# Block sums of the squared activations in a two-layer encoder: made beside the up projection and stored as finished operands, or made again from stored activations beside the down projection

## The chip, the cores and the metric

One of the eight cores of a Trainium2 chip runs the whole program. The metric is device time in microseconds from launch to end, and lower is better. The kernel before was run three times: 2643.0 us is the median, 2638.96 us the lowest. A further execution was recorded by the hardware profiler; the rows below come from it.

## What is computed

The reference is a two-layer encoder for 1024 tokens of width 1024. Layer 0 mixes tokens by banded attention, layer 1 by a gated delta rule. Each layer then adds a dense MLP with a squared ReLU; the change lies in these two MLPs alone.

```python
def squared_relu_mlp(h, w_up, w_down):          # w_up 1024 x 4096, w_down 4096 x 1024
    return jnp.square(jax.nn.relu(h @ w_up)) @ w_down
...
x = x + squared_relu_mlp(rmsnorm(x, mlp_norm[i]), mlp_w_up[i], mlp_w_down[i])
```

All of it is float32. The kernel reaches that precision on TensorE by writing each operand as a high part (rounded to the fp32r format) plus a low part (the rest), and multiplying high by high, high by low and low by high. So one product of two 128-wide operands is three matmuls (`block_product`, L998), and every operand needs a "high" (a ScalarE copy with rounding, `high`, L1012) and a "low" (a subtraction, `low`, L1006, on VectorE, or on GpSimd where its last argument is true).

## The kernel before

Everything is kept transposed: features on the 128 partitions, the 1024 tokens along the free dimension in two halves of 512. A tile of 128 features by 1024 tokens is 512 KB, one half of it 256 KB.

Both projections use the seven-product form of a 2x2 block product (eight products in the plain form). For the right-hand operand with blocks 11, 12, 21, 22 (first digit the half of the features, second the half of the tokens) this needs 11, 21 and 22 themselves and four block sums: t1 = 12 - 11, t2 = 22 - t1, t3 = 22 - 12, t4 = 21 - t2. The weights have their own sums s1 to s4. Results gather in PSUM banks called X (in the trace `acc`), Y and Z.

**Up projection** (`up`, L1077). Sixteen steps n; step n makes two tiles of 128 rows of h @ w_up, numbers 2n and 2n+1, in seven block products of 12 matmuls each, in the order 11, t1, t2, 21, t3, 22, t4 of the right-hand operand (from the second step on; the last has t4 before 22). While TensorE works on step n, the other engines make the weight operands of step n+1 (`up_weights`, L1026): GpSimd four sums and differences, ScalarE the highs, VectorE the lows. Bank Y takes the products 11, t2, t3 and t4 one on top of the other and is read out after each, so the next product into Y has to wait for that reading: after 11 and t2 by a ScalarE copy (`copy`, L1104, into a tile `nt`), after t3 and t4 by VectorE (`put`, L1082). `put` makes a result: VectorE adds the copied bank (L1087), then takes the ReLU and multiplies by the norm's factor R (L1089), ScalarE squares (L1090) and sends the 256 KB to DRAM (L1091, tensor `gd`). The buffers of the results are four halves called `ssum` and `g` in the trace.

**Down projection** (`down`, L1313). The 4096 rows of the activations form 8 blocks b of four tiles; each block times four pairs of output tiles u gives 32 units of seven block products of 6 matmuls. `slot` (L1366) is one product: the matmuls, then `step` (L1328), then a VectorE add of the bank onto the running result x in SBUF (L1369). Bank Y again holds four products, so the add after a product stands between it and the next product into the same bank, with one product of another bank in between to cover it. `step` advances two helpers by one stage each: `rows` (L1264), which prepares the activation operands of block b+1, and `down_weights` (L1173), which prepares the weight operands of the next unit. All engines run their own instructions strictly in program order; what `step` emits comes ahead of the add of the same slot.

`rows` loads the four 256 KB blocks 11, 12, 21, 22 from `gd`, and for each of the two tile rows j of a block makes the four sums on GpSimd (`psub`, L1015, which the trace shows at L1016), seven highs on ScalarE, and seven lows, four on VectorE and three (`PLO`, L28) on GpSimd. It takes 14 slots for one j, that is two units. `first_rows` (L1237) does the same for block 0 during the last step of the up projection, called by `tail` (L1485) in `block` (L1467), which also reloads the residual tiles x0 and x1 early and x2 to x7 at its end.

TensorE, VectorE, ScalarE and GpSimd follow the order in which the code is written (`manual_schedule`, L1500). SyncE only issues loads and stores; a scheduler orders its queue by when it takes the buffers to be free, and it waits at each entry until that entry's data and buffer are ready.

## Time and profile before

| What | Value |
|---|---|
| Median of three runs | 2643.0 us (lowest 2638.96) |
| The profiled execution | 2639.7 us |
| Span in the profile, first to last instruction | 2637.9 us (1.8 us lie outside) |
| Mean granted TensorE clock | 0.983 of full speed |
| TensorE busy | 2492.1 us, 94% of the span |
| VectorE, ScalarE, GpSimd busy | 72%, 46%, 50% |
| Moved by DMA | 271.78 MB, mean 103 GB/s |
| Up projections | about 561 to 891 us and 1953 to 2282 us |
| Down projections | about 891 to 1234 us and 2282 to 2622 us |

Times inside the trace count from the span's start. "Busy" is the time in which at least one instruction of an engine ran. A matmul's end is modelled and overlaps the start of the next, so idle time of PE in brackets is somewhat less than what a wait really cost; the distance between the starts of two matmuls shows the whole. PE is TensorE, DVE VectorE, ACT ScalarE, POOL GpSimd, SP SyncE; L161 is a recording helper that stands for many lines.

### The profile page before, as it was taken

The numbers are of one execution on the slowest core, as the hardware profiler recorded it, in microseconds if no ns is written. First come the engines' busy times: TensorE is split into PE (matmuls) and PEld (weight loads), VectorE is DVE, ScalarE is ACT, GpSimd is POOL, SyncE is SP. The second block draws the span as 40 slices with busy tenths as digits, with TensorE's granted clock in tenths as the row PEclk, the third lists the DMA queues.
The fourth block names the chain that finished last, engine by engine and source line by source line (L and its number), as shares of the span: only waits on it lengthen the run. The fifth ranks groups of instructions, "written<-read, shape, count | busy, mean of one in ns | idle before, by whom it ended". The sixth has DMA issues, their size and how long they took to land.

```text
span 2637.9 us, 36117 instructions
## 1 busy us (share of the span) xinstructions
PE 2492.1 (94%) x12638; PEld 2061.5 (78%) x12638; DVE 1886.2 (72%) x3287; ACT 1225.0 (46%) x2269; POOL 1310.9 (50%) x1100
## 2 busy tenths in 40 slices
PE   8999999989999999998888999999899999999997
PEld 6888888867888777776677788888777888777775
DVE  6665656575454899997579976666676545899997
ACT  6665667443444444434673343343334434444443
POOL 2444456242222788886464333332133232688886
PEclk9999999999999999999998999999999999999998
DMA  4222225324333423323443122223323323432322
GB/s 159 67 70 72 68 84 164 104 80 142 114 105 119 152 96 108 100 88 114 115 140 111 54 73 65 67 72 108 108 96 132 116 104 120 153 103 97 103 97 80
DMA packets 141814, 271.78 MB, mean 103 GB/s; under 512 B 49264, under 2 KB 55856, under 8 KB 141632
## 3 DMA queue, kind: packets, MB, share of 16 engines
q1 hardware_dynamic: 120752, 227.51, 27.0%
q10 hardware_dynamic: 20880, 41.97, 4.1%
q8 instruction: 99, 1.62, 0.3%
q14 instruction: 83, 0.68, 0.1%
HBM read 193.24 MB, written 67.80 MB: 99 GB/s over the span
## 4 chain that ended last, share of the span: by engine, by line
PE 70%; DVE 18%; issue 6%; ACT 3%; DMA 2%; POOL 1%; SPq 0%; ACTq 0%; DVEq 0%; POOLq 0%
PE y L1004 20%; PE acc L161 17%; PE z L1004 9%; PE acc L1004 6%; PE tp L161 3%; DVE x L1369 3%; DVE a L1010 3%; PE s L161 3%; PE po L161 2%; PE pt L161 2%; PE sp L161 2%; PE acc L276 2%; PE acc L277 2%; PE acc L275 2%; DVE ft L161 2%
## 5 line engine op out<-in xcount | busy, mean ns | idle before, releaser
L161 PE MATMUL acc<-xhi,whi 128*128 128x512 f32 (+1 forms) x904 | 372.8, 412 | 7.2 <-DVE xp L161 7.2
L161 PE MATMUL acc<-xlo,whi 128*128 128x512 f32 (+1 forms) x904 | 371.7, 411 | 0.6 <-DVE xlo L391 0.6
L161 PE MATMUL acc<-xhi,wlo 128*128 128x512 f32 x896 | 368.0, 411 | 2.8 <-POOL wlo L161 2.8
L1019 POOL TENSOR_TENSOR s<-wraw 128x256 f32<-128x256 f32 (+1 forms) x93 | 101.3, 1089 | 538.6 <-DMA wraw<-in_w_up_dram 380.0
L161 POOL TENSOR_TENSOR wlo<-wraw,whi 128x512 fp32r<-128x512 f32 x126 | 168.1, 1334 | 242.8 <-ACT whi L161 193.8
L1013 ACT ACTIVATE xhi<-r 128x512 fp32r<-128x512 f32 x224 | 135.9, 628 | 261.5 <-POOL r L1016 210.0
L1010 DVE TENSOR_TENSOR wlo<-wraw,whi 128x512 fp32r<-128x512 f32 (+1 forms) x184 | 203.4, 1105 | 50.8 <-ACT whi L1013 47.5
L1004 PE MATMUL y<-xhi,a 128*128 128x512 f32 x488 | 181.3, 412 | 33.1 <-DVE x L1369 30.4
L1004 PE MATMUL y<-xhi,wlo 128*128 128x512 f32 x504 | 200.1, 397 | 13.1 <-DVE wlo L1010 13.1
L1004 PE MATMUL y<-xhi,whi 128*128 128x512 f32 x504 | 200.3, 397 | 11.6 <-DVE ssum L1087 9.1
L1016 POOL TENSOR_TENSOR r<-r,r 128x512 f32<-128x512 f32 x124 | 204.1, 1648 | 13.6 <-DVE xlo L1010 13.3
L1004 PE MATMUL y<-xlo,whi 128*128 128x512 f32 x504 | 199.2, 395 | 0.0
L161 PEld LDWEIGHTS acc<-xhi,whi 128*128 128x128 f32 (+1 forms) x904 | 172.2, 190 | 31.9 <-DVE xp L161 4.4
L161 PEld LDWEIGHTS acc<-xhi,wlo 128*128 128x128 f32 x896 | 171.1, 191 | 28.4 <-POOL wlo L161 4.1
L161 PEld LDWEIGHTS acc<-xlo,whi 128*128 128x128 f32 (+1 forms) x904 | 172.5, 191 | 24.9 <-DVE xlo L391 1.2
L1369 DVE TENSOR_TENSOR x<-y,x 128x512 f32<-128x512 f32 x240 | 163.6, 682 | 8.9 <-PE y L1004 8.5
L1013 ACT ACTIVATE whi<-wraw 128x512 fp32r<-128x512 f32 (+2 forms) x191 | 143.7, 766 | 35.1 <-ACT g L1090 12.3
L1004 PEld LDWEIGHTS y<-xhi,a 128*128 128x128 f32 x488 | 92.0, 189 | 80.1 <-DVE x L1369 60.1
L161 POOL TENSOR_SCALAR pr<-pr,rs 128x640 f32<-128x640 f32 (+4 forms) x128 | 88.6, 696 | 128.9 <-DVE rs L161 97.9
L1087 DVE TENSOR_TENSOR ssum<-acc,nt 128x512 f32<-128x512 f32 x32 | 22.1, 690 | 175.7 <-PE acc L1004 175.7
L161 POOL TENSOR_TENSOR cy<-cy,cz 128x512 f32<-128x512 f32 x48 | 68.9, 1436 | 145.1 <-DVE cz L161 131.2
L1010 DVE TENSOR_TENSOR a<-s,a 128x256 fp32r<-128x256 f32 x117 | 129.7, 1109 | 0.0
(349 smaller groups left out, 7089.3 us busy)
## 6 DMA issues: line engine op xcount, KB each, us to landing
wraw<-in_w_up_dram SPq DMA_DIRECT2D x64, 512.0 KB, 3.3
wraw<-in_w_down_dram SPq DMA_DIRECT2D x64, 512.0 KB, 3.9
r<-gd SPq DMA_DIRECT2D x112, 256.0 KB, 2.7
gd<-ssum ACTq DMA_DIRECT2D x64, 256.0 KB, 2.0
gd<-g ACTq DMA_DIRECT2D x64, 256.0 KB, 2.2
wraw<-in_w_in_dram SPq DMA_DIRECT2D x32, 512.0 KB, 3.5
wraw<-in_w_qkv_dram SPq DMA_DIRECT2D x30, 512.0 KB, 3.4
x<-xd SPq DMA_DIRECT2D x24, 512.0 KB, 5.1
```

Of the source, the lines that this page charges most:

```text
L161: return call(*args, **more)
L275: nc.tensor.matmul(ps, hi[:, k], xh, start=(k == 0), stop=False)
L276: nc.tensor.matmul(ps, hi[:, k], xl, start=False, stop=False)
L277: nc.tensor.matmul(ps, lo[:, k], xh, start=False, stop=(k == KT - 1))
L1004: nc.tensor.matmul(ps, w[:, k], x, start=bool(first and f), stop=bool(last and e), skip_group_check=True)
L1010: self.nc.vector.tensor_tensor(lo, src, hi.bitcast(F32), ALU.subtract)
L1013: self.nc.scalar.activation(hi, src, AF.Copy)
L1016: self.nc.gpsimd.tensor_tensor(out, x, y, ALU.subtract)
L1019: self.nc.gpsimd.tensor_tensor(out, x, y, ALU.add)
L1087: nc.vector.tensor_tensor(g, c, t, ALU.add)
L1369: nc.vector.tensor_tensor(x, ps, x, ALU.add)
```

## The change

Both halves of an up step now belong to one pair of blocks: the halves of a down block are its even and its odd tiles (the reordering of w_down in `layout`), so that step n of the up projection makes all four blocks of one tile row j. A new generator `combine` makes the four sums of step n beside step n+1: GpSimd subtracts, ScalarE makes the high part, VectorE the low part in place, and one 512 KB store per sum puts high and low, side by side, into the DRAM tensor `gt`. Blocks 11, 21 and 22 are stored as before (tensor `gr`); block 12 is no longer stored. In the down projection `rows` loads the raw 11, 21 and 22 and makes their highs on ScalarE and all their lows on GpSimd; the sums are loaded straight into the operand tiles, two loads of 256 KB each. `first_rows` does likewise. High and low of an operand are now two halves of one tile. The sums of the last up step are made in the first slots of the down projection, and the residual tiles are loaded later: x0 to x3 at the end of `tail`, x4 to x7 behind those last sums.

```diff
+    def combine(self, n, g, mp, gt):
+        t = {z: mp.tile([P, S], F32, name=self.nm("c"), tag=f"x{4 * (n % 2) + k}") for k, z in enumerate(SUMS)}
+        def sub(z, x, y):
+            self.psub(t[z][:, HB:], x, y)
+        def high(z):
+            self.high(t[z][:, :HB].bitcast(F32R), t[z][:, HB:])
+        def low(z):
+            nc.vector.tensor_tensor(t[z][:, HB:].bitcast(F32R), t[z][:, HB:], t[z][:, :HB], ALU.subtract)
+            nc.sync.dma_start(gt[n, SUMS.index(z)], t[z])
+        sub("t1", g[0, 1], g[0, 0])
+        sub("t3", g[1, 1], g[0, 1])
+        yield
+        sub("t2", g[1, 1], t["t1"][:, HB:])
+        sub("t4", g[1, 0], t["t2"][:, HB:])
+        high("t1")
+        yield
+        high("t3")
+        low("t1")
+        yield
+        high("t2")
+        low("t3")
+        yield
+        high("t4")
+        low("t2")
+        yield
+        low("t4")
+        yield
...
-            nc.scalar.dma_start(gd[m, :, s], g)
+            g_of[m % 2, h] = g
+            if (m % 2, h) in RAW:
+                nc.scalar.dma_start(gr[m // 2, RAW.index((m % 2, h))], g)
...
+                next(sums)
                 self.block_product(Z, A["s1"], ops["t1"], True, False)
                 next(rest, None)
                 beside(1, lambda: next(more, None), lambda: copied("z5", Z))
+                next(sums)
                 end()
                 self.block_product(Y, A["s2"], ops["t2"], False, False)
                 copied("u2", Y)
+                next(sums)
                 end()
                 self.block_product(X, A["12"], ops["21"], True, True)
                 beside(2, lambda: next(more, None), lambda: put(2 * n, 0, X, keep["p1"]))
+                next(sums)
                 self.block_product(Y, A["s3"], ops["t3"], False, False)
                 beside(3, lambda: (next(more, None), end()), lambda: put(2 * n + 1, 1, Y, keep["z5"]))
+                next(sums)
...
+            sums = self.combine(n, dict(g_of), mp, gt)
+            if n < last:
+                next(sums)
...
+    def load_sum(self, part, src):
+        hi, lo = part
+        self.nc.sync.dma_start(hi.bitcast(F32), src[:, :HB])
+        self.nc.sync.dma_start(lo.bitcast(F32), src[:, HB:])
+    def rows(self, hx, gr, gt, b, ops):
         for j in range(2):
+            n = 2 * b + j
+            r = {}
+            for k, name in enumerate(RAWS):
+                r[name] = hx.tile([P, HB], F32, name=self.nm("r"), tag=f"a{6 + k}")
+                self.nc.sync.dma_start(r[name], gr[n, k])
+            yield
+            for k, name in enumerate(RAWS):
+                self.high(self.rows_part(hx, ops, b, name, j)[0], r[name])
+                yield
                 h, l = ops[name][j]
+                self.low(l, r[name], h, True)
+                yield
+            yield
+            for k, name in enumerate(SUMS):
+                self.load_sum(self.rows_part(hx, ops, b, name, j), gt[n, k])
+                yield
+            yield
+            yield
...
-                got["xs"] += self.load_x(xp, xd, range(2, KT))
+                got["xs"] = self.load_x(xp, xd, range(4))
+                yield
+            def late():
+                for k in range(4, KT):
+                    got["xs"] += self.load_x(xp, xd, (k,))
...
-    o["w_down"] = np.ascontiguousarray(w.transpose(0, 1, 5, 4, 6, 2, 3, 7)).reshape(2, 8, 4, P, 4, 2, P)
+    o["w_down"] = np.ascontiguousarray(w.transpose(0, 1, 5, 4, 6, 3, 2, 7)).reshape(2, 8, 4, P, 4, 2, P)
```

TensorE's instructions and their order are the same in both kernels, and over the whole program VectorE, GpSimd and ScalarE execute the same number of highs, lows and subtractions. What differs is where they stand. Three places follow. In their rows a name's number only tells buffers apart, and a line number belongs to the kernel that the row is from.

VectorE in one step of the up projection, before, from the result of product 21 to the lows of the next weights:

```order
L1087 TENSOR_TENSOR ssum_6920<-acc_8069,nt_8086 128x512
L1089 SCALAR_TENSOR_TENSOR ssum_6920<-ssum_6920,R_6907 128x512
L1087 TENSOR_TENSOR ssum_6920<-y_8070,nt_8105 128x512
L1089 SCALAR_TENSOR_TENSOR ssum_6920<-ssum_6920,R_6907 128x512
L1010 TENSOR_TENSOR alo_8137<-s_8133,ahi_8136 128x512
L1010 TENSOR_TENSOR wlo_8143<-wraw_8101,whi_8142 128x1024
L1087 TENSOR_TENSOR g_6921<-z_8071,nt_8119 128x512
L1089 SCALAR_TENSOR_TENSOR g_6921<-g_6921,R_6907 128x512
```

The same place after, with the two rows ahead of it; c is a tile of a sum, in the order t1, t3, t2, t4:

```order
L1093 TENSOR_TENSOR c_8164<-c_8164 128x512
L1093 TENSOR_TENSOR c_8166<-c_8166 128x512
L1127 TENSOR_TENSOR ssum_6864<-acc_8170,nt_8187 128x512
L1129 SCALAR_TENSOR_TENSOR ssum_6864<-ssum_6864,R_6851 128x512
L1093 TENSOR_TENSOR c_8165<-c_8165 128x512
L1127 TENSOR_TENSOR ssum_6864<-y_8171,nt_8209 128x512
L1129 SCALAR_TENSOR_TENSOR ssum_6864<-ssum_6864,R_6851 128x512
L1093 TENSOR_TENSOR c_8167<-c_8167 128x512
L1014 TENSOR_TENSOR alo_8247<-s_8243,ahi_8246 128x512
L1014 TENSOR_TENSOR wlo_8253<-wraw_8205,whi_8252 128x1024
L1127 TENSOR_TENSOR g_6865<-z_8172,nt_8226 128x512
L1129 SCALAR_TENSOR_TENSOR g_6865<-g_6865,R_6851 128x512
```

Four lows have come into the step: two while VectorE has nothing else to do, and two (t2 and t4) between the results of products 21 and 22.

GpSimd in two units of the down projection, before (s and wraw: weights; r: raw blocks; xlo: the low part of an activation operand):

```order
L1016 TENSOR_TENSOR r_9513<-r_9514,r_9513 128x512
L1008 TENSOR_TENSOR xlo_9572<-r_9513,xhi_9571 128x512
L1016 TENSOR_TENSOR r_9514<-r_9516,r_9514 128x512
L1008 TENSOR_TENSOR xlo_9595<-r_9514,xhi_9594 128x512
L1016 TENSOR_TENSOR r_9513<-r_9516,r_9513 128x512
L1019 TENSOR_TENSOR s_9617<-wraw_9600 128x256
L1016 TENSOR_TENSOR s_9618<-s_9617,wraw_9600 128x256
L1016 TENSOR_TENSOR r_9515<-r_9515,r_9513 128x512
L1016 TENSOR_TENSOR s_9617<-wraw_9600 128x256
L1016 TENSOR_TENSOR wraw_9600<-wraw_9600,s_9618 128x256
L1008 TENSOR_TENSOR xlo_9665<-r_9515,xhi_9664 128x512
```

And after, where two units hold these (xs is an operand's tile of high and low):

```order
L1023 TENSOR_TENSOR s_9721<-wraw_9700 128x256
L1020 TENSOR_TENSOR s_9722<-s_9721,wraw_9700 128x256
L1012 TENSOR_TENSOR xs_9732<-r_9712,xs_9732 128x512
L1020 TENSOR_TENSOR s_9721<-wraw_9700 128x256
L1020 TENSOR_TENSOR wraw_9700<-wraw_9700,s_9722 128x256
L1012 TENSOR_TENSOR xs_9755<-r_9714,xs_9755 128x512
L1012 TENSOR_TENSOR xs_9773<-r_9716,xs_9773 128x512
L1023 TENSOR_TENSOR s_9804<-wraw_9789 128x256
L1020 TENSOR_TENSOR s_9805<-s_9804,wraw_9789 128x256
L1020 TENSOR_TENSOR s_9804<-wraw_9789 128x256
L1020 TENSOR_TENSOR wraw_9789<-wraw_9789,s_9805 128x256
```

The four subtractions r<-r,r are gone from the two units; the three lows remain, now of the raw blocks. VectorE's four lows of activations are gone too, so that between its seven adds of a unit only the four lows of the weights stand.

SyncE's queue around the end of the first up projection, before: the loads of the first two down weights, one raw block for block 1, and residual tiles x2 to x5 (x0 and x1 were loaded 300 us earlier):

```order
L1031 DMA wraw_8798<-in_w_up_dram 128x1024
L1176 DMA wraw_8923<-in_w_down_dram 128x1024
L1176 DMA wraw_9125<-in_w_down_dram 128x1024
L1270 DMA r_9137<-gd_6121 128x512
L2449 DMA x_9117<-xd_6122 128x1024
```

And after, where c_9114, c_9113 and c_9115 are the sums t3, t2, t4 of the last but one up step, xs_9284 and xs_9287 the operands t4 of block 0, x_9314 to x_9320 the residual tiles x0 to x3, and wraw_9322 the weights of the second unit:

```order
L1094 DMA gt_6090<-c_9114 128x1024
L1337 DMA xs_9284<-gt_6090 128x512
L1094 DMA gt_6090<-c_9113 128x1024
L1338 DMA xs_9284<-gt_6090 128x512
L1337 DMA xs_9287<-gt_6090 128x512
L1094 DMA gt_6090<-c_9115 128x1024
L1338 DMA xs_9287<-gt_6090 128x512
L2505 DMA x_9314<-xd_6091 128x1024
L2505 DMA x_9316<-xd_6091 128x1024
L2505 DMA x_9318<-xd_6091 128x1024
L2505 DMA x_9320<-xd_6091 128x1024
L1227 DMA wraw_9322<-in_w_down_dram 128x1024
```

The residual tiles and the second unit's weights have come behind the stores of sums and the loads of operands.

## Rows read from the trace of the kernel before

**Rows 1.** The page: each engine's busy time with its share of the span and its instructions, and the chain of work that ended last, by engine.

```profile
PE 2492.1 (94%) x12638; PEld 2061.5 (78%) x12638; DVE 1886.2 (72%) x3287; ACT 1225.0 (46%) x2269; POOL 1310.9 (50%) x1100
PE 70%; DVE 18%; issue 6%; ACT 3%; DMA 2%; POOL 1%; SPq 0%; ACTq 0%; DVEq 0%; POOLq 0%
```

**Rows 2.** Busy time by stretch: an up and a down stretch of 50 us in the first MLP. Columns: length; PE, PEld, DVE, ACT, POOL busy with their instructions; granted clock, DMA share, GB/s.

```profile
750.00:800.00 50.00, 50.00 (x223) 41.40 (x222) 25.17 (x32) 20.81 (x33) 10.79 (x9) 1.00 0.35 122
1000.00:1050.00 50.00, 48.09 (x207) 38.07 (x206) 46.37 (x64) 20.39 (x37) 43.58 (x36) 1.00 0.29 95
```

**Rows 3.** Who waited for whom over the whole span: us in total, times, the longest.

```profile
POOL s L1019 <- DMA wraw<-in_w_up_dram: 380.0, 28, 17.9
ACT xhi L1013 <- POOL r L1016: 210.0, 112, 2.2
...
PE y L1004 <- DVE x L1369: 33.0, 34, 2.1
```

**Rows 4.** TensorE's timeline: start, duration, instruction, in brackets the idle time before it and what ended it. First the starts of product 11 in two successive up steps and of product t2 in the second of them; then product t2 in five units of the two down projections (the first unit and the 28th of each, and two units that lie two apart).

```profile
696.18 0.39 PE L1004 MATMUL y<-xhi,whi 128*128 128x512 f32 x1
...
715.22 0.39 PE L1004 MATMUL y<-xhi,whi 128*128 128x512 f32 x1
...
720.66 0.39 PE L1004 MATMUL y<-xhi,ahi 128*128 128x512 f32 x1
...
896.26 0.50 PE L1004 MATMUL y<-xhi,a 128*128 128x512 f32 x1 [2.04 <-DVE x L1369]
...
989.44 0.50 PE L1004 MATMUL y<-xhi,a 128*128 128x512 f32 x1 [0.84 <-DVE x L1369]
...
1010.21 0.50 PE L1004 MATMUL y<-xhi,a 128*128 128x512 f32 x1 [0.84 <-DVE x L1369]
...
1176.35 0.50 PE L1004 MATMUL y<-xhi,a 128*128 128x512 f32 x1 [0.84 <-DVE x L1369]
...
2287.36 0.50 PE L1004 MATMUL y<-xhi,a 128*128 128x512 f32 x1 [2.04 <-DVE x L1369]
...
2566.91 0.50 PE L1004 MATMUL y<-xhi,a 128*128 128x512 f32 x1 [0.84 <-DVE x L1369]
```

**Rows 5.** VectorE's timeline just ahead of the product at 989.44, then one ScalarE row of the same moment and the start of TensorE's product before it.

```profile
985.16 1.58 DVE L1010 TENSOR_TENSOR a<-s,a 128x512 fp32r<-128x512 f32 x1
986.66 0.68 DVE L1369 TENSOR_TENSOR x<-y,x 128x512 f32<-128x512 f32 x1
987.49 1.29 DVE L1010 TENSOR_TENSOR wlo<-wraw,whi 128x512 fp32r<-128x512 f32 x1
988.70 0.68 DVE L1369 TENSOR_TENSOR x<-y,x 128x512 f32<-128x512 f32 x1
...
986.23 0.63 ACT L1013 ACTIVATE xhi<-r 128x512 fp32r<-128x512 f32 x1 [2.13 <-POOL r L1016]
...
987.07 0.39 PE L1004 MATMUL z<-xhi,a 128*128 128x512 f32 x1
```

**Rows 6.** Groups of instructions of VectorE and GpSimd from 947.4 to 1196.6 us, six blocks of the first down projection: count, busy us, mean ns of one, idle time before them.

```profile
L1369 DVE TENSOR_TENSOR x<-y,x 128x512 f32<-128x512 f32 x97 | 66.1, 682 | 2.0 <-PE y L1004 1.9
L1010 DVE TENSOR_TENSOR wlo<-wraw,whi 128x512 fp32r<-128x512 f32 x46 | 46.1, 1002 | 1.6
L1010 DVE TENSOR_TENSOR a<-s,a 128x512 fp32r<-128x512 f32 x22 | 34.1, 1548 | 0.0
...
L1016 POOL TENSOR_TENSOR r<-r,r 128x512 f32<-128x512 f32 x46 | 76.4, 1661 | 0.0
```

**Rows 7.** The same view from 640 to 840 us, in the first up projection: lows of weight sums on VectorE, and sums of weights on GpSimd.

```profile
L1010 DVE TENSOR_TENSOR alo<-s,ahi 128x512 fp32r<-128x512 f32 x32 | 22.0, 688 | 4.5 <-ACT ahi L1013 4.5
...
L1016 POOL TENSOR_TENSOR s<-s,wraw 128x512 f32<-128x512 f32 x11 | 14.2, 1292 | 0.9
```

**Rows 8.** Timeline of one up step: four results on VectorE, and ScalarE's copy of the next step's product 11.

```profile
708.04 1.22 DVE L1089 SCALAR_TENSOR_TENSOR ssum<-ssum,R 128x512 f32<-128x512 f32 x1
710.04 0.69 DVE L1087 TENSOR_TENSOR ssum<-y,nt 128x512 f32<-128x512 f32 x1 [0.78 <-PE y L1004]
710.76 0.69 DVE L1089 SCALAR_TENSOR_TENSOR ssum<-ssum,R 128x512 f32<-128x512 f32 x1
...
715.42 0.69 DVE L1089 SCALAR_TENSOR_TENSOR g<-y,R 128x512 f32<-128x512 f32 x1 [0.30 <-PE y L1004]
...
718.25 0.58 ACT L1106 ACTIVATE nt<-y 128x512 f32<-128x512 f32 x1
```

**Rows 9.** Timeline of the last two up steps of the first MLP, where the subtractions of `first_rows` run on GpSimd: VectorE, then the waits of TensorE up to the down projection.

```profile
860.36 1.63 DVE L1089 SCALAR_TENSOR_TENSOR ssum<-ssum,R 128x512 f32<-128x512 f32 x1
...
869.35 1.78 DVE L1010 TENSOR_TENSOR alo<-s,ahi 128x512 fp32r<-128x512 f32 x1
...
874.47 0.50 PE L1004 MATMUL y<-xhi,ahi 128*128 128x512 f32 x1 [1.33 <-ACT nt L1106]
...
881.18 0.50 PE L1004 MATMUL y<-xhi,ahi 128*128 128x512 f32 x1 [0.98 <-ACT nt L1106]
...
885.76 0.50 PE L1004 MATMUL y<-xhi,whi 128*128 128x512 f32 x1 [1.56 <-DVE ssum L1087]
```

**Rows 10.** DMA: the stretch around the start of the first down projection (columns as in Rows 2), and the page's line on the loads of residual tiles (KB each, median us from issue to landing).

```profile
883.00:900.00 17.00, 13.40 (x53) 10.34 (x52) 15.52 (x24) 9.95 (x19) 4.53 (x5) 0.93 0.83 292
...
x<-xd SPq DMA_DIRECT2D x24, 512.0 KB, 5.1
```

130 lines of the change are left out of this document (55 added, 75 removed).

## The prediction

> **What bounds the kernel now.** I read the page first. TensorE is busy 94% of the span and makes 70% of the chain that ended last; VectorE makes 18% of it [rows 1]. Those are averages over stages, so I went on to busy time by stretch. In an up stretch TensorE is busy 50.00 of 50 us, with VectorE at 25 and GpSimd at 11. In a down stretch it is busy 48.1, while VectorE stands at 46.4 and GpSimd at 43.6 [rows 2]. So the up projections are bound by matmuls with room beside them, and the down projections sit at a place where three engines are almost full. The view of waits names the pair: TensorE's product into Y waits for VectorE's add onto x, 33.0 us in 34 waits [rows 3].
>
> How much that costs is read better from starts of matmuls than from the idle times, since a matmul's end is modelled. An up step has 84 matmuls and takes 715.22 - 696.18 = 19.04 us, 0.2267 us each [rows 4]. Two down units also have 84, and there the same product returns after 1010.21 - 989.44 = 20.77 us [rows 4]: 1.73 us are lost in each pair of units. From the first unit's t2 product to the 28th's lie 27 units, 1134 matmuls, 257.0 us at the up pitch; the trace shows 1176.35 - 896.26 = 280.1 in the first MLP and 2566.91 - 2287.36 = 279.6 in the second [rows 4]. The losses are 23.0 and 22.5, together 45.6 us. This is all that a better down projection could return in the stretch that the change touches; the last block, which prepares no rows, is not in it.
>
> Why the add is late is seen just ahead of 989.44 [rows 5]. VectorE takes the low of the weights s3 and s1 in 1.58 us, adds, waits, takes another low in 1.29 and only then adds what TensorE waits for. Where GpSimd rests, such a low takes 0.69 [rows 7]; in the down projection the two sorts average 1.55 and 1.00 beside GpSimd's subtractions of 1.66 us [rows 6]. An add that reads a PSUM bank stays at 0.68 there [rows 6]. ScalarE is held as well: it stands 210 us behind those subtractions [rows 3], one of them 2.13 us ahead of the very high whose low is late [rows 5].
>
> **The change, part by part.** *Down projection.* For two units it removes four subtractions of 1.66 us (6.6) from GpSimd, four lows of 0.68 (2.7) from VectorE, four highs from ScalarE, and with them the wait of ScalarE for GpSimd. What remains on VectorE in one unit is seven adds and four lows, 7 x 0.68 + 3 x 0.69 + some 0.4 for the half-sized one, 7.2 us of the 9.5 that TensorE needs. I put the sequence of [rows 5] together again with a low of 0.69: start 985.16, end 985.85; the add follows; the next low, no longer kept by ScalarE, ends about 987.3 to 987.7, and the awaited add at 988.0 to 988.4. The product was due at 988.43, six matmuls of 0.2267 behind the start of the one before at 987.07 [rows 5]. So the wait goes, with little to spare; GpSimd still has the weight sums there. I let nine tenths of the loss go: -41. The ends are -23, if contention with the three remaining lows and the weight sums keeps half of it, and -45.6.
>
> *Loads.* For two units the loads rise from eight blocks of 256 KB to three and four sums of 512 KB, 2.75 MB, plus 1 MB of weights, 3.75 MB in 19 us or about 205 GB/s; the up step stores as much beside its 1 MB of weights. The queues moved 292 GB/s around 890 us with a share of 0.83 [rows 10], so there is room, and most of these loads are issued a whole block ahead. Nothing, with the price of a late one in the rivals.
>
> *Up projection.* Steps 1 to 15 gain four subtractions, four highs and four lows each. GpSimd has idle time for four times 1.29 to 1.66: it waits 380 us in 28 steps, 13.6 each, for the next weights [rows 3]. Two lows fall where VectorE has nothing to do. The other two, t2 and t4, lie on a path that ends at ScalarE's copy of the next step's product 11, since results, squares and that copy follow each other in order. That copy ran at 718.25 to 718.83 and TensorE wanted it at 720.66: 1.83 spare [rows 4, 8]. VectorE itself waits for TensorE on that path for 0.78 and 0.30 [rows 8], so 2.91 us can be added unseen. Added are 2 x 0.69 = 1.38 at best. The weight loads come free later behind the longer VectorE work, so GpSimd's four weight operations move onto the results and the low of t2: then that low takes 1.78 for 0.69, and the two rescalings 1.63 for 1.22 and 0.69 [rows 8, 9], together 1.09 + 0.41 + 0.94 more, 3.82 in all, 0.9 too much. I take a value near the middle, some 2.9 to 3.1, and 0.15 us in 28 steps: +4. The ends are 0 and, by the nearest row in which subtractions lie on this very path, 1.33 of idle time [rows 9].
>
> Here the Trainium skill has a rule (SBUF — State Buffer, section "SBUF: two separate sides"): VectorE with two SBUF inputs and GpSimd share a port pair under an exclusive lock, and the loser is blocked for the winner's whole instruction. The lows of 1.78 against 0.69, and the adds from PSUM that stay at 0.68, agree with it [rows 6, 7, 9]. By that rule each of the three instructions on the path could wait out a whole subtraction, and the result would be the second rival.
>
> *The passage from up to down.* TensorE lost 1.33, 0.98, 1.56 and 2.04 there [rows 4, 9]. The first shrinks, since the eight early subtractions go, the third by about one low of 0.69. Against that the sums of the last step put four lows into the first unit, and x0 to x3 and the second unit's weights come behind stores. x0 is issued when the low of t4 is stored, some 2 us behind 885.76, and lands 5.1 later [rows 9, 10], about 893, ahead of the add that released 896.26. The second unit's weights land a few us behind that, about 896 to 897, and VectorE's low of them stands ahead of three adds of the first unit: some 2 us. I take +1 for each passage, +2, with ends -6 and +10.
>
> Sum: the profiled execution took 2639.7 us, 2637.9 of span and 1.8 outside, 0.1% below the median of the runs. 2639.7 - 41 + 4 + 2 = 2604.7, rounded to 2605.
>
> **Rivals.** *Half comes back.* The wait moves to another low: the low of 22 on GpSimd beside the low of s3 and s1, or weights that land behind 2 MB of sums in SyncE's queue and hold ScalarE. For it: the 1.15 to 1.29 lows of the second weight half lie beside weight sums that stay. Against it: GpSimd's work in two units falls by 6.6 of about 18 us. Then 2639.7 - 23 + 6 = about 2623.
>
> *Slower: the subtractions bring their lock into the up steps.* Place: ScalarE's copy of product 11 ahead of the t2 product; price 1.33 of idle time and about 0.2 of refill, 1.5 in each of 28 steps, 42 us. It decides from the point where the added path exceeds 2.91 us, and outweighs the gain when a step loses over 1.35. Then 2639.7 - 41 + 2 + 44 = about 2645. For it: the last step of before shows it. Against it: that step had eight subtractions and two lows of 1.75 and 2.31 on the path, and a lost microsecond moves TensorE away from GpSimd's operations, so the loss limits itself.
>
> *More than the sum.* All 45.6 come back and the passages shrink too: about 2588.
>
> **How the numbers follow.** Chances: the forecast, 2593 to 2617, 0.68; half back, 0.14; slower, 0.10; more, 0.08. A measurement of this kernel can tell about 2% from no change, here 53 us. A gain of over 2% would need the whole loss of the down projections and more: 0.06. A loss of over 2% needs two bad cases together: 0.02. The range from 2590 to 2638 leaves out the worst of the second rival and part of the last.
>
> **What would show it.** In the profile after: down stretches with TensorE at 49.5 or more of 50 us, GpSimd at 25 to 30 and VectorE near 40; the same product returning after 19.1 to 19.4 us; lows near 0.7. Up stretches still at 50.00 with the step at 19.04 to 19.3 us; a wait of TensorE for ACT nt in every step would mean the second rival. At the start of the down projection, waits up to 3 us. The prediction is wrong if pairs of units still take over 20 us, or if up steps take over 19.5.

## The result, and the profile after

The changed kernel takes 2614.3 us (median of four runs, 2608.4 to 2616.4), the kernel before beside it 2642.2: a ratio of 0.9895, 95% interval 0.9873 to 0.9917. One of the four runs of the kernel before took 4961.2 us, far from the other three (2638.96 to 2643.0); without it the median is 2641.4. The changed kernel is faster by 1.0%. The interval ends below 1, but the gain is under the 2% that the prediction set as what a measurement can tell. The forecast of 2605 was 9 us too low. The profiled execution took 2614.5 us with a span of 2612.4; before it was 2637.9, so 25.5 us went.

The page of the kernel after, the two rows that answer to [rows 1], busy time and the chain that ended last:

```profile
PE 2476.4 (95%) x12638; PEld 2067.2 (79%) x12638; DVE 1922.9 (74%) x3287; ACT 1211.8 (46%) x2269; POOL 1320.8 (51%) x1100
...
PE 76%; DVE 12%; DMA 4%; issue 3%; POOL 2%; ACT 2%; SPq 1%; DVEq 0%; ACTq 0%; POOLq 0%
```

In the chain VectorE fell from 18 to 12% and DMA rose from 2 to 4%. The busy shares moved by a point or two and tell little. The view of windows tells more (columns as in [rows 2]): an up stretch, a down stretch, and the passage from the one to the other, whole and at its worst.

```profile
700.00:750.00 50.00, 50.00 (x220) 40.90 (x220) 39.96 (x40) 25.42 (x42) 36.27 (x23) 1.00 0.51 195
1000.00:1050.00 50.00, 50.00 (x222) 41.39 (x221) 41.16 (x59) 15.69 (x29) 32.31 (x33) 1.00 0.58 187
870.00:930.00 60.00, 48.15 (x190) 37.82 (x190) 39.87 (x56) 24.52 (x44) 33.43 (x28) 0.91 0.93 351
890.00:900.00 10.00, 7.20 (x24) 5.14 (x22) 2.59 (x4) 0.65 (x2) 2.49 (x2) 0.83 1.03 413
900.00:910.00 10.00, 5.27 (x13) 4.16 (x14) 7.43 (x10) 6.05 (x11) 9.53 (x8) 0.66 0.61 247
```

TensorE now fills both the up and the down stretch. The trouble is between them. From 870 to 930 us it is busy 48.15 of 60, and the DMA engines work at a share of 0.93 with 351 GB/s. The same 60 us of the kernel before:

```profile
870.00:930.00 60.00, 53.31 (x222) 41.97 (x221) 53.35 (x73) 30.69 (x55) 39.97 (x34) 0.97 0.47 164
```

So the DMA share in the passage doubled from 0.47 to 0.93, and TensorE lost 5.2 us of work in that stretch.

Starts of matmuls cut the whole span into stretches that hold the same matmuls in both kernels. From TensorE's timeline of the kernel after, these are starts in the first MLP: the product t1 of the last up step, t2 and t3 of the first down unit, then t2 of the second, fifth and 28th unit ([rows 4] has t2 of the first and the 28th of before). All but the t3 at 904.73 are borders of stretches; that one is shown for its wait.

```profile
870.04 0.39 PE L1008 MATMUL z<-xs,ahi 128*128 128x512 f32 x1
...
895.18 0.50 PE L1008 MATMUL y<-xs,a 128*128 128x512 f32 x1 [2.58 <-DVE x L1419]
...
904.73 0.80 PE L1008 MATMUL y<-xs,a 128*128 128x512 f32 x1 [4.95 <-DVE x L1419]
...
913.94 0.39 PE L1008 MATMUL y<-xs,a 128*128 128x512 f32 x1
...
944.96 0.39 PE L1008 MATMUL y<-xs,a 128*128 128x512 f32 x1
...
1163.92 0.39 PE L1008 MATMUL y<-xs,a 128*128 128x512 f32 x1
```

| Stretch (us; first MLP / second MLP) | Before | After | Both together |
|---|---|---|---|
| 15 up steps, t1 of step 1 to t1 of step 16 | 287.21 / 285.68 | 286.12 / 286.27 | -0.5 |
| Passage: on to t2 of down unit 5 (252 matmuls, 57.1 at the up pitch) | 67.33 / 66.85 | 74.91 / 72.37 | +13.1 |
| 23 down units, t2 of unit 5 to t2 of unit 28 | 238.76 / 238.78 | 218.96 / 218.96 | -39.6 |
| All else (ahead of, between and behind) | | | +1.5 |

The table is the result in short. The 23 middle units take 218.96 us for 966 matmuls in both MLPs, 0.2267 each, the up pitch: nothing at all is lost there. A third of that gain is given back in the passage.

The view of waits, over the whole span, answers to [rows 3]:

```profile
POOL c L1020 <- ACT g L1130: 179.4, 31, 11.1
...
DVE c L1093 <- POOL c L1020: 35.7, 30, 1.2
...
POOL s L1023 <- DMA wraw<-in_w_up_dram: 24.1, 27, 5.7
PE y L1008 <- DVE x L1419: 22.9, 12, 5.0
```

TensorE's waits for the add went from 34 to 12: eight in the two passages, up to 5.0 us long, and four in the first MLP's last block, from 1187 us on, which prepares no rows. GpSimd's 380 us of waiting for the next up weights shrank to 24. It still has idle time in the up steps, busy 36.27 of 50 us, but it now spends most of it waiting for ScalarE's square of the step's last results (ACT g, 179.4 us). And a new wait came, of VectorE for GpSimd, 1.19 us in each of 30 steps; it is taken up below.

Why the add is no longer late stands in the groups of VectorE from 947.4 to 1160 us, which answer to [rows 6]:

```profile
L1419 DVE TENSOR_TENSOR x<-y,x 128x512 f32<-128x512 f32 x89 | 61.4, 690 | 12.1 <-PE y L1008 8.4
L1014 DVE TENSOR_TENSOR wlo<-wraw,whi 128x512 fp32r<-128x512 f32 x44 | 47.0, 1068 | 0.0
...
L1014 DVE TENSOR_TENSOR a<-s,a 128x512 fp32r<-128x512 f32 x22 | 15.0, 683 | 0.0
```

The low of s3 and s1 fell from 1548 to 683 ns. The adds wait for TensorE now, where TensorE waited for them. The other low stays at 1068 ns beside GpSimd's remaining work, and harms nobody.

What happens in the passage is seen in the timelines of SyncE, VectorE and ScalarE (the number behind a row's start is its duration; SPq rows are issues):

```profile
886.89 5.41 SPq L2505 DMA_DIRECT2D x<-xd  x4
892.35 0.43 SPq L1227 DMA_DIRECT2D wraw<-in_w_down_dram  x1
...
894.43 0.69 DVE L1419 TENSOR_TENSOR x<-y,x 128x512 f32<-128x512 f32 x1 [2.50 <-DMA x<-xd]
900.84 0.69 DVE L1014 TENSOR_TENSOR wlo<-wraw,whi 128x512 fp32r<-128x512 f32 x1 [5.72 <-ACT whi L1017]
901.45 0.68 DVE L1419 TENSOR_TENSOR x<-z,x 128x512 f32<-128x512 f32 x1
903.38 0.69 DVE L1093 TENSOR_TENSOR c<-c 128x512 fp32r<-128x512 f32 x1 [1.25 <-POOL c L1020]
903.99 0.68 DVE L1419 TENSOR_TENSOR x<-y,x 128x512 f32<-128x512 f32 x1
...
900.18 0.63 ACT L1017 ACTIVATE whi<-wraw 128x512 fp32r<-128x512 f32 x1 [8.18 <-DMA wraw<-in_w_down_dram]
```

x0 is issued at 886.89, and the first add starts 7.5 us later, at 894.43. The second unit's weights are issued at 892.35 and reach ScalarE at 900.18. VectorE's low of them and the low of sum t1 (c) stand ahead of two adds, and TensorE starts again at 904.73. Meanwhile SyncE issues nothing from 895.72 to 904.10, since the next entry of its queue is the store of sum t1, which waits for that low (SyncE's waits from 895 to 905 us):

```profile
SPq L1094 <- DVE c L1093: 7.1, 1, 7.1
```

With nothing issued, the DMA share falls to 0.61 from 900 to 910 us. The loads of x4 to x7 and of the fourth unit's weights stand behind that store.

### The profile page after: what moved, and what is told of

Same layout as the page of the kernel before. It is cut to its first block, busy times and chain, and to the rows that moved or that the text cites. A ratio compares the mean times of both kernels' runs of the same rounds, so it can differ in the third digit from the quotient of the medians.

```text
span 2612.4 us, 36716 instructions
## 1 busy us (share of the span) xinstructions
PE 2476.4 (95%) x12638; PEld 2067.2 (79%) x12638; DVE 1922.9 (74%) x3287; ACT 1211.8 (46%) x2269; POOL 1320.8 (51%) x1100
## 4 chain that ended last, share of the span: by engine, by line
PE 76%; DVE 12%; DMA 4%; issue 3%; POOL 2%; ACT 2%; SPq 1%; DVEq 0%; ACTq 0%; POOLq 0%
PE y L1008 23%; PE acc L164 17%; PE z L1008 11%; PE acc L1008 6%; PE tp L164 3%; PE s L164 3%; PE po L164 2%; PE pt L164 2%; PE sp L164 2%; PE acc L279 2%; PE acc L280 2%; PE acc L278 2%; DVE ft L164 2%; DVE wlo L1014 1%; DMA xs<-gt 1%
## 5 line engine op out<-in xcount | busy, mean ns | idle before, releaser
L164 PE MATMUL acc<-xs,whi 128*128 128x512 f32 x1808 | 629.1, 411 | 9.7 <-DVE xp L164 7.2
L164 PEld LDWEIGHTS acc<-xs,whi 128*128 128x128 f32 x1808 | 331.6, 190 | 59.0 <-DVE xp L164 7.9
L164 PE MATMUL acc<-xs,wlo 128*128 128x512 f32 x896 | 367.0, 410 | 2.8 <-POOL wlo L164 2.8
L1008 PE MATMUL y<-xs,whi 128*128 128x512 f32 x1008 | 316.9, 396 | 9.2 <-DVE ssum L1127 9.2
L1008 PEld LDWEIGHTS y<-xs,whi 128*128 128x128 f32 x1008 | 192.9, 192 | 51.0 <-DVE ssum L1127 10.4
L1008 PE MATMUL y<-xs,a 128*128 128x512 f32 x732 | 192.0, 398 | 22.9 <-DVE x L1419 22.9
L1008 PE MATMUL y<-xs,wlo 128*128 128x512 f32 x504 | 200.0, 397 | 12.9 <-DVE wlo L1014 12.9
L164 PEld LDWEIGHTS acc<-xs,wlo 128*128 128x128 f32 x896 | 170.7, 190 | 28.3 <-POOL wlo L164 4.4
L1093 DVE TENSOR_TENSOR c<-c 128x512 fp32r<-128x512 f32 x128 | 151.9, 1206 | 36.2 <-POOL c L1020 35.7
L1008 PE MATMUL acc<-xs,whi 128*128 128x512 f32 x528 | 164.2, 392 | 0.0
L1008 PE MATMUL y<-xs,ahi 128*128 128x512 f32 x512 | 158.6, 391 | 2.0 <-ACT nt L1148 2.0
L1020 POOL TENSOR_TENSOR c<-g,ssum 128x512 f32<-128x512 f32 x32 | 41.4, 1295 | 184.4 <-ACT g L1130 179.4
```

Of the source, the lines that this page charges most:

```text
L164: return call(*args, **more)
L1008: nc.tensor.matmul(ps, w[:, k], x, start=bool(first and f), stop=bool(last and e), skip_group_check=True)
L1020: self.nc.gpsimd.tensor_tensor(out, x, y, ALU.subtract)
L1093: nc.vector.tensor_tensor(t[z][:, HB:].bitcast(F32R), t[z][:, HB:], t[z][:, :HB], ALU.subtract)
```

## The experiments

Three questions were put: whether GpSimd's subtractions were what the down projection lost its time to; what exactly costs the passage 8 and 6 us; and how near the second rival was. Times are medians of four runs (five for the version with the new order of the subtractions), ratios are to the kernel before on the same chip. The changed kernel stands at 2614.3; its passages at 74.91 and 72.37 us by the table's second row. It was not run beside the versions below, and runs of one kernel differ by up to 8 us, so that differences of 2 or 3 us between medians tell little by themselves. A passage is read from one profiled execution, but between the starts of the same matmuls.

### Down projection: subtractions or lows

**The kernel before without the four subtractions.** In `rows` the four `self.psub(...)` go; raw blocks stand in for the sums.

> The kernel before, without GpSimd's four subtractions for each tile row in the down projection (raw blocks stand in for the sums, so that part of the computation is left out); highs, lows and loads stay as they are, VectorE's four lows of activations too. Theory D (the 45.6 us were lost because VectorE's lows and ScalarE's highs ran beside or waited for those subtractions): 35 to 44 us less than before, 2598 to 2607. Rival E (VectorE simply had too many lows): 10 to 20 less, 2622 to 2632.

Measured: 2599.7 us, ratio 0.9839 (0.9821 to 0.9857). Theory D. The 23 middle units take 218.96 us in both MLPs: the whole loss goes, with VectorE's own lows all still there.

**The kernel before without VectorE's four lows.**

```diff
-                self.low(l, src, h, name in PLO)
+                if name in PLO:
+                    self.low(l, src, h, True)
+                else:
+                    ops[name][j] = (h, h)
```

> The kernel before, with GpSimd's subtractions kept but without VectorE's four lows of activations for each tile row in the down projection (the high part stands in for the low; part of the computation is left out). Theory D: the weights' lows still take 1.0 to 1.55 us beside the subtractions and ScalarE still waits for GpSimd; 10 to 25 less than before, 2617 to 2632. Rival E: 35 to 45 less, 2597 to 2607.

Measured: 2616.4 us, ratio 0.9908 (0.9892 to 0.9924); the middle units 228.01 and 228.72. Half a microsecond under theory D's range, and far from rival E: half of the loss goes, half stays. The groups of VectorE from 947.4 to 1160 us, first without the subtractions, then without the lows:

```profile
L1010 DVE TENSOR_TENSOR wlo<-wraw,whi 128x512 fp32r<-128x512 f32 x44 | 37.2, 846 | 0.0
L1010 DVE TENSOR_TENSOR xlo<-r,xhi 128x512 fp32r<-128x512 f32 x45 | 30.5, 679 | 0.0
...
L1010 DVE TENSOR_TENSOR a<-s,a 128x512 fp32r<-128x512 f32 x22 | 17.7, 803 | 0.0
```

```profile
L1010 DVE TENSOR_TENSOR a<-s,a 128x512 fp32r<-128x512 f32 x22 | 21.0, 956 | 0.0
```

Without the subtractions the low of s3 and s1 takes 803 ns for the 1548 of [rows 6]; without VectorE's lows it is still 956. The window from 1000 to 1050 us without the subtractions:

```profile
1000.00:1050.00 50.00, 50.00 (x223) 41.40 (x222) 46.04 (x70) 21.21 (x40) 33.15 (x30) 1.00 0.36 118
```

VectorE is as busy as in [rows 2], 46.04 of 50 us, and TensorE does not wait. A busy share of 92% was not the limit; what stood ahead of the adds, the longer lows and ScalarE's wait, was. The two gains, 41 and 24, together exceed the 45.6 that were lost: either part lowers the other's cost.

### The passage: order, bytes or work

**Second unit's weights first; x0 first; both.** In `tail`, ahead of the loads of t4:

```diff
+                    if k == 2:
+                        got["nxt"] = {}
+                        got["more"] = self.down_weights(i, 0, 1, hx, got["nxt"])
+                        next(got["more"])
+                    if len(got["xs"]) == 0 and got["k"] == 3:
+                        got["xs"] = self.load_x(xp, xd, range(1))
+                    got["k"] += 1
```

> The changed kernel, with the load of the second down unit's weights issued in the last up step, ahead of the store of sum t2, the operand loads of t4 and the residual tiles x0 to x3 (in the changed kernel it stands behind all of them and lands at about 900 us). Theory A (the passage lost some 8 us in each MLP because these weights and x0 land late): the wait of 4.95 us on the add onto x at 904.73 goes, the wait of 2.58 for x0 at 895.18 stays; 5 us for each MLP, 2604 us (2601 to 2609). Rival B (the last step's sums, four lows on VectorE and four subtractions, hold the adds of the first unit): no more than 2 us, 2612 to 2616. Rival C (the DMA engines are full there, and what is loaded earlier only makes another load late): 2611 to 2617, with x0 or the third unit's weights later by as much.

> The changed kernel, with the load of x0 alone issued earlier, ahead of the store of sum t2 and the operand loads of t4; the second unit's weights stay where they are. Theory A: the wait of 2.58 us at 895.18 goes, but the low of the second unit's weights still waits until 900 us ahead of the next adds, so the wait there grows by as much: 2614 us (2611 to 2616). If the waits simply add up: 5 us less, 2609. Rival B: 2614. Rival C: 2614 to 2617.

> The changed kernel with both moves: the second unit's weights and x0 issued in the last up step. Theory A: both waits go, 7.5 us for each MLP, 2600 us (2596 to 2605). Rival B: 2612 to 2616. Rival C: 2609 to 2617, with waits of the same total at other loads.

Measured, in this order: 2610.2 us (ratio 0.9876, 0.9861 to 0.9891), 2614.2 (0.9892, 0.9876 to 0.9909) and 2610.4 (0.9879, 0.9864 to 0.9893). The second came as theory A said: x0 alone is swallowed by the weights. The other two gave 4 us where 10 and 15 were expected, so A alone does not hold. By the two passages together, 147.3 us in the changed kernel, the three take 142.4, 147.1 and 145.1. Why is seen with both moved (the profiled execution, 2616.0 us, is the slowest of its four), first VectorE, then ScalarE, then TensorE:

```profile
896.07 0.69 DVE L1417 TENSOR_TENSOR x<-z,x 128x512 f32<-128x512 f32 x1 [3.69 <-DMA x<-xd]
...
922.02 0.63 ACT L1017 ACTIVATE whi<-wraw 128x512 fp32r<-128x512 f32 x1 [7.55 <-DMA wraw<-in_w_down_dram]
...
924.63 0.50 PE L1008 MATMUL y<-xs,a 128*128 128x512 f32 x1 [3.01 <-DVE x L1417]
```

The next tile x1 is late in place of x0, and later the fourth unit's weights. A wait that was taken away by reordering moved to what was put behind.

**Without the last step's sums, and with the sums but without their stores.** In `up` the last `combine` goes, or in `combine` the store stands under `if n < 15`; block 7 loads the sums of step 14.

> The changed kernel without the four sums of the last up step (block 7 loads the sums of the step before in their place, so part of the computation is left out). Theory A: the second unit's weights and x0 still land where they did, 2612 us (2608 to 2615). Rival B: the 8 us of each passage go, 2598 to 2604. Rival C: some 2 MB of stores less behind the passage, 2608 to 2614.

> The changed kernel, in which the last up step's four sums are made as before but not stored (left out are their four stores of 512 KB for each MLP; block 7 loads the sums of the step before). Theory C (the passage is bound by DMA: the share of the DMA engines is 0.98 to 1.05 from 870 to 930 us, at 350 to 413 GB/s): as without the sums, 2606 us (2602 to 2609). Rival B (VectorE and GpSimd making those sums are the cost): as the changed kernel, 2614 (2612 to 2616).

Measured: 2605.7 (0.9858, 0.9843 to 0.9873) without the sums, 2611.8 (0.9889, 0.9871 to 0.9906) without the stores alone. Against A, which gave the sums 2 us, they cost some 9; by the passages, 140.1 without the sums and 144.3 without the stores for 147.3, they cost 7, and the stores 3 of that. C took the engines to be full from 870 to 930 us, but the share was 0.61 from 900 to 910. The stores begin at 904 us, behind both waits; without them the fourth unit's weights are in time, and a third wait of TensorE, 1.55 us at 927.90 in the changed kernel, is gone. Making the sums is the larger part, which C does not explain (x4 to x7, which need their buffers, also come earlier without them; that share was not separated). But in the first MLP the two waits for late loads stay without the sums, as A said: 2.63 us at 894.65, and

```profile
902.19 0.79 PE L1008 MATMUL y<-xs,a 128*128 128x512 f32 x1 [4.53 <-DVE x L1419]
```

**Fewer bytes in the passage.** `load("t1")` is issued two steps earlier.

> The changed kernel, with block 0's loads of sum t1 (four of 256 KB, into tiles that nothing else uses) issued two up steps earlier, where the DMA share is about 0.6; nothing is left out. Theory C: 1 MB less in the full stretch, at some 380 GB/s 2.8 us for each MLP: 2609 us (2606 to 2612). Theory A alone (it is only the order of SyncE's queue for two loads): 2614, and B: 2614 (2612 to 2616).

Measured: 2614.8 us (0.9901, 0.9885 to 0.9917), no change; the waits in the first MLP stay at 2.58 and 4.74 us, and x0 still lands 7.5 us after its issue. Moving 1 MB out of the full stretch does nothing while the late loads keep their places in the queue. Theory C in its strong form falls.

**Everything in order of need.** x0 takes the buffer that comes free first (`XTAG = (7, 0, 1, 3, 4, 5, 6, 2)`), x1 the next; the second and third unit's weights are issued earlier; block 1's first highs start two slots later.

> The changed kernel with the loads of the passage from up to down in the order in which they are needed, and nothing left out: residual tile x0 takes the buffer that is free first (that of sum t4 of the step before the last but one) and x1 that of sum t1, both issued in the last up step, as are the second unit's weights; the third unit's weights are issued ahead of the first unit; and the highs of block 1's first tile row start two slots later, so that ScalarE does not wait for their loads. The last step's sums use other buffers but stand in the same slots. Theory F (what was seen so far: moving one load ahead made the next one late, x1 and the third unit's weights, since the DMA engines are full; so all have to be moved by need): the waits for x0, x1 and both weights go, 5 to 7 us for each MLP, 2603 us (2598 to 2607). Rival B (making the last sums in the first unit is most of the cost): 2609 to 2613. Rival C in its strong form (bytes alone decide): 2610 to 2616.

Measured: 2608.5 us (0.9873, 0.9857 to 0.9889): 6 us, passages 71.15 and 69.97, short of theory F and half a microsecond under rival B's range. What is left stands in its timeline, VectorE first, then GpSimd, then TensorE:

```profile
897.34 0.69 DVE L1096 TENSOR_TENSOR c<-c 128x512 fp32r<-128x512 f32 x1 [3.29 <-POOL c L1023]
897.95 0.68 DVE L1421 TENSOR_TENSOR x<-y,x 128x512 f32<-128x512 f32 x1
...
891.61 1.28 POOL L1023 TENSOR_TENSOR c<-g,ssum 128x512 f32<-128x512 f32 x1 [11.17 <-DMA xs<-gt]
892.86 1.74 POOL L1023 TENSOR_TENSOR c<-ssum,g 128x512 f32<-128x512 f32 x1
894.55 0.73 POOL L1026 TENSOR_TENSOR s<-wraw 128x256 f32<-128x256 f32 x1
895.36 0.72 POOL L1023 TENSOR_TENSOR s<-s,wraw 128x256 f32<-128x256 f32 x1
896.04 1.26 POOL L1023 TENSOR_TENSOR c<-ssum,c 128x512 f32<-128x512 f32 x1
...
898.69 0.50 PE L1011 MATMUL y<-xs,a 128*128 128x512 f32 x1 [3.55 <-DVE x L1421]
```

In the first unit no DMA is late any more (the fourth unit's weights still are, 3.03 us at 922.78). The 11.17 us ahead of GpSimd's first subtraction are put down to a load, but the square that it reads ends only 0.08 us before it, at 891.53. VectorE's low of t1 waits 3.29 us for a subtraction of GpSimd: `low` overwrites t1 in place, and t2 = 22 - t1 still reads it. That subtraction stands behind t3's and two weight sums. In this run it is that wait, not the low itself, that holds the add. It is the wait of 1.19 us that the kernel after has in every up step, where it is hidden.

**The same with the sums spread over ten slots.**

> The kernel of e7b_order_by_need with the last step's sums spread over ten slots of the first two units, one stage in every second slot, in place of five slots. Theory F: the lows of the sums do not stand together ahead of the first adds any more, 0 to 2 us less than e7b for each MLP unless the later loads of x4 to x7 are late; 2601 us (2597 to 2606). Rival B: 3 to 4 us less than e7b for each MLP.

Measured: 2615.5 us (0.9904, 0.9887 to 0.9921), 7 slower than in five slots; passages 74.56 and 74.72. Both numbers were wrong; what happened is the exception that theory F named. x4 to x7 share buffers with the sums and are issued later, the last at 914 us; the fourth unit's weights come behind them, at 916.7 for 912.5, and TensorE waits 6.10 us at 926.36 for 3.03 at 922.78.

**Order of need, and t2 subtracted right behind t1.** The kernel with everything in order of need and the sums in five slots, with the fourth unit's weights issued ahead of the second unit, and with this order in the last step's `combine` (the steps before keep theirs; the branch that tells them apart is left out here):

```diff
         sub("t1", g[0, 1], g[0, 0])
-        sub("t3", g[1, 1], g[0, 1])
+        sub("t2", g[1, 1], t["t1"][:, HB:])
         yield
-        sub("t2", g[1, 1], t["t1"][:, HB:])
+        sub("t3", g[1, 1], g[0, 1])
         sub("t4", g[1, 0], t["t2"][:, HB:])
```

> The kernel of e7b_order_by_need with two more moves, nothing left out: for the last step's sums GpSimd subtracts t2 right behind t1 and t3 after that, so that VectorE's low of t1, which overwrites t1 in place, no longer waits for the subtraction of t2 that still reads it (idle 3.29 us there in e7b, and TensorE 3.55); and the fourth unit's weights are issued ahead of the second unit, in front of the operand loads of block 1 (in e7b they land at 920 us and TensorE waits 3.03 at 922.78). Theory F and this reading: both waits fall by 2 us or more in each MLP, 2599 us (2595 to 2604). Rival C (bytes alone decide; a wait of the same size appears at another load): 2606 to 2610. Rival B (the lows themselves hold the adds, not that wait): the first wait stays above 2.5 us, 2604 to 2608.

Measured: 2601.4 us (2600.2 to 2602.7), ratio 0.9847, interval 0.9833 to 0.9860, the best version here, 13 us under the changed kernel and with the whole computation. Its passages take 66.83 and 66.38 us, those of before 67.33 and 66.85. The window over its passage:

```profile
870.00:930.00 60.00, 52.41 (x224) 41.13 (x223) 47.12 (x65) 25.50 (x46) 38.29 (x33) 1.00 0.99 366
```

VectorE's low of t1 in its timeline, then two waits of TensorE in the first unit, ahead of its products t3 and t4:

```profile
894.10 1.21 DVE L1096 TENSOR_TENSOR c<-c 128x512 fp32r<-128x512 f32 x1 [0.58 <-POOL c L1023]
...
895.96 1.66 PE L1011 MATMUL y<-xs,a 128*128 128x512 f32 x6 [1.34 <-DVE x L1427]
901.66 0.73 PE L1011 MATMUL y<-xs,whi 128*128 128x512 f32 x2 [2.68 <-DVE x L1427]
```

The low starts 3.24 us earlier than with everything in order of need. The DMA share is 0.99, higher than in the changed kernel, and TensorE is busy 4.3 us more. So it was not the bytes that lengthened the passage: with all of them it is back at its old length, by order alone.

Starts of the same matmuls tell where it came back (us, first MLP / second MLP):

| From | To | Before | Changed | Order of need | This run |
|---|---|---|---|---|---|
| t1 of up step 16 | t2 of unit 1 | 26.00 / 26.08 | 25.14 / 24.72 | 22.39 / 22.01 | 21.92 / 22.40 |
| t2 of unit 1 | t2 of unit 2 | 11.65 / 10.36 | 18.76 / 17.98 | 15.12 / 15.10 | 14.83 / 14.83 |
| t2 of unit 3 | t2 of unit 4 | 10.39 / 10.66 | 11.80 / 10.48 | 14.49 / 13.68 | 10.90 / 9.97 |

A unit without a wait takes 9.52 us. The changed kernel lost 7.1 and 7.6 us over before between t2 of units 1 and 2. Loads in order of need gave 3.6 and 2.9 of that back, the new order of the subtractions only 0.3 each: its expectation held for the time, but the first unit's wait of 3.55 us became two of 1.34 and 2.68. Of this run's gain of 7.9 us in the two passages over order of need, 7.3 lie between units 3 and 4, where the fourth unit's weights had been late. From t2 of unit 1 to t2 of unit 2 it is still 5.3 us too long, although the loads that were late there are in time; the lows of the last sums stand between the adds, and rival B is not refuted for that part. The passage is back at its old length because the stretch ahead of unit 1, where x0 now lands in time, is 4.1 and 3.7 us shorter than before. A run with the loads in order and without the last sums was not made. The 9.7 and 9.3 us by which these passages still exceed the up pitch were not looked into.

### How near the second rival was

**Each subtraction beside the up projection twice.** In `combine`, `for _ in range(2): self.psub(...)`.

> The changed kernel with each of GpSimd's subtractions for the sums beside the up projection done twice (same result): four more of about 1.3 to 1.7 us in each of 30 steps and in the first down unit. Forecast's up term (GpSimd has 13.6 us of idle time in a step and VectorE 2.9 us of room): 2614 to 2622, an up step of 19.04 to 19.3 us. The second rival of the prediction (their lock brings VectorE past its room and ScalarE's copy of product 11 late): 1.3 us or more in each step, 2650 to 2665, with a wait of TensorE for nt in every step.

Measured: 2744.7 us, ratio 1.0395 (1.0377 to 1.0413). Both expectations were far too low. The first 15 up steps of the first MLP take 22.83 us each in the mean for 19.07. The timeline of a step, VectorE and TensorE:

```profile
702.42 2.39 DVE L1094 TENSOR_TENSOR c<-c 128x512 fp32r<-128x512 f32 x2 [5.17 <-POOL c L1020]
...
706.43 1.78 DVE L1094 TENSOR_TENSOR c<-c 128x512 fp32r<-128x512 f32 x1
...
711.54 1.77 DVE L1014 TENSOR_TENSOR alo<-s,ahi 128x512 fp32r<-128x512 f32 x1
713.23 1.21 DVE L1014 TENSOR_TENSOR wlo<-wraw,whi 128x1024 fp32r<-128x1024 f32 x1
...
714.50 0.50 PE L1008 MATMUL y<-xs,wlo 128*128 128x512 f32 x1 [2.17 <-DVE wlo L1014]
```

The low of t1 waits 5.17 us for the subtraction of t2, the next three lows of half a tile run at 1.77 to 1.78 us beside GpSimd, and the next weights' low is late for TensorE. The eight subtractions take some 12.5 us in a step (two each of 1457, 1779, 1293 and 1710 ns in the mean) where the four took 7.1 (means of 1296, 1746, 2275 and 1798 ns from 640 to 840 us); of the 5.4 us more, 3.8 show. So the up steps of the changed kernel had some 1.6 us of room left, an estimate from these two runs that takes each further microsecond to show in full, and not the idle time of GpSimd that [rows 3] shows.

The changed kernel's own trace tells of less room, and at the place that the second rival named: ScalarE's copy of product 11, and the product t2 that waits for it.

```profile
719.39 0.58 ACT L1148 ACTIVATE nt<-y 128x512 f32<-128x512 f32 x1
...
720.02 0.50 PE L1008 MATMUL y<-xs,ahi 128*128 128x512 f32 x1
```

The copy ends 0.05 us ahead of the product, where 1.83 were spare in the step of [rows 4, 8]. From the third step on it is 0.05 to 1.04 us ahead, in both MLPs. In four steps of the first MLP it is 0.05 or 0.06; these take 19.16 to 19.27 us for 19.04.

## Why the prediction was right, and where its sum was not

**Down projection: right, and a little small.** The loss of 45.6 us, read from starts of matmuls, was the right quantity, and the cause (GpSimd's subtractions lengthen VectorE's lows and hold ScalarE) is shown by taking the subtractions away alone. Of the 39.6 lost in the 23 middle units all came back, where nine tenths, 35.7, were forecast. Half back, the first rival, did not happen. Whether the longer lows or ScalarE's wait weighed more was not separated. The lows took 1548 ns with the subtractions and 683 to 803 without, and adds that read PSUM 0.68 to 0.69 throughout. In the kernel before, the low of 1.58 us at 985.16 [rows 5] meets the second of these rows of GpSimd:

```profile
974.90 1.30 POOL L1008 TENSOR_TENSOR xlo<-r,xhi 128x512 fp32r<-128x512 f32 x1
...
984.91 1.29 POOL L1016 TENSOR_TENSOR r<-r,r 128x512 f32<-128x512 f32 x1
```

It ends 0.54 us behind that subtraction, and so, by 0.54 or 0.55, do all 15 such lows from 954 to 1102 us behind the instruction on GpSimd that they meet. That agrees with the rule that the prediction cited. The Trainium skill (SBUF — State Buffer, "SBUF: two separate sides") states it as an exclusive lock, held for the winner's whole instruction. In 8 of the 15, as in the first row above, that instruction is not a subtraction but one of GpSimd's own lows. Without the subtractions those lows are all still there, and VectorE's takes 803 ns in the mean; so the subtractions did part of their harm by where they put them.

**Loads: "so there is room" was wrong for the passage.** The estimate of 205 GB/s was made for a steady unit; the trace shows 187 there, near enough. In the passage the operands of two blocks, the tiles x0 to x7 and the last stores fall together, and the trace shows up to 413 GB/s at a share of 1.03, which leaves the engines next to no room from 890 to 900 us. The Trainium skill (DMA: Bandwidth & Descriptors, "Specifications") gives 435 GB/s as the ceiling of the fabric. The trace agrees so far that no stretch read here is above it.

**Up projection: +4 forecast, -0.5 measured.** From the second step on, the steps stayed at 19.04 to 19.27 us. The low of the sums takes 1.21 us in the mean and waits for GpSimd, and TensorE is held for some 0.1 to 0.2 us in four steps. That is the second rival's mechanism at its own place, ScalarE's copy of product 11, without its price of 1.5 us a step: the path was at its limit, as the prediction's 2.9 to 3.1 for 2.91 had it, and the term of 0.15 us in 28 steps was too much. (The middle of the prediction's two values, 1.38 and 3.82, is 2.60; and the rival's sum takes 44 us for a price given as 42.) With the subtractions doubled the step is 3.8 us longer, and there the loss shows first at a place that was not named, the low of the next weights ahead of product 11.

**The passage: the step that failed.** The prediction took +2 for both, with ends of -6 and +10, and put x0 at 893 and the second unit's weights at 896 to 897. They came at 894.4 and 900.2, since loads land 7.5 to 7.8 us after their issue there and not 5.1. Behind them the lows of the last sums, with VectorE's wait of 1.25 us for the subtraction of t2, held adds; the prediction had named four such lows and given them no time of their own. By the table the passage with its first four units was to change by 2 - 0.9 x 5.9 = -3.3 us (5.9 is what those four units lost before: 41.33 + 40.77 for 2 x 38.09) and changed by +13.1. That is 16.4 too little, a term of +18 in place of +2, outside its ends. The other differences (-3.9 in the down units, -4.5 in the up steps, +1.5 elsewhere) took 6.9 of it back, which is why the total was only 9 us off. That these errors had opposite signs is luck.

That this term is not one of bytes is shown: the version with the new order of the subtractions has the passage back at the length of before with all its bytes. How it divides between late loads and late sums in the changed kernel is shown only roughly. It lost 14.7 us between t2 of units 1 and 2, more than in the whole passage; 7.1 of them came back by order and 7.7 did not. Leaving out the sums alone gave 7 to 9 us in all, and the two overlap.

Of the signs that the prediction named, the down and up stretches at 50.00 of 50 us and the returning product, 19.04 us, came about as said (19.1 to 19.4 was expected for the product). GpSimd is busy 32.3 us in a down stretch for the 25 to 30 expected, one kind of low takes 1.07 us for 0.7, and the waits at the start of the down projection reach 4.95 us for the 3 expected. That last one is the passage again.

## What to carry to other kernels

When work is moved out of a crowded stage, look at the border to it: what must be loaded there, in which order the queue issues it, which store at the head of the queue waits for work, and what is left to compute there. A load that is late in a full queue is mended by the order of need, with all that follows it, and not by one move. When two moves bring a gain together, the starts of the same matmuls tell where it came. The room on a path is read from the last instruction before the engine that must not wait, not from an engine's idle time.

## What was not expected of the hardware

In the changed kernel's passage, at a DMA share near 1.0, loads and stores of 256 to 512 KB took 5 to 9 us from issue to landing; a store of a sum, issued at 904.10, landed after 2.6 us when the share was 0.61 for a moment. TensorE's granted clock fell from 1.00 to a mean of 0.83 from 890 to 900 us and of 0.66 from 900 to 910, after TensorE had waited (2.4 GHz is the upper level, 1.2 the lower). The six matmuls from 904.73 on took 2.73 us to the start of the next product, where 1.36 is the up pitch. With shorter waits, in the version with the new order of the subtractions, the clock stayed at 1.00 over the whole passage. So part of what a wait costs is paid behind it. And eight subtractions in place of four cost 130 us on an engine that is busy for 51% of the changed kernel's span.
